# State-space stage of a hybrid decoder layer: B is turned on VectorE in the wide stage and loaded turned, instead of being turned on TensorE in each step

## The chip, the cores and the metric

The kernel runs on one core of one Trainium2 chip. A core has a matrix engine (TensorE, "PE" in the profile, with its weight loads as "PEld"), a vector engine (VectorE, "DVE"), an engine for activations and scaled copies (ScalarE, "ACT"), a general engine (GpSimd, "POOL"), a sequencer that here only issues DMAs (SyncE, "SP"), and 16 DMA engines between them. Each engine works through its own queue in order; semaphores connect the queues. ScalarE also issues DMAs, and each of these takes a place in its queue. The metric is the device time of one execution in microseconds; less is better.

## The reference

One layer over a sequence of S = 1024 positions and D = 1024 channels in float32. A normalised and modulated input `h` is multiplied by one wide matrix `w_in`; its columns feed a chunked gMLP mixer, a Mamba-2 state-space mixer and two gates. The part that matters here:

```
proj = h @ w_in
gm_u, gm_v, gm_z, ssm_z, xbc, dt_raw, g_a, g_b = split(proj)
xbc = silu(causal_depthwise_conv(xbc, conv_w, conv_b))      # 4 taps
xs, bm, cm = split(xbc)                                     # x: 2048, B: 8*128, C: 8*128
# state space, per chunk of 128 positions, 8 groups of 4 heads:
cb           = einsum('bclgn,bcsgn->bcgls', cc, bc)
y_diag       = einsum('bcgls,bcgrls,bcsgrp->bclgrp', cb, decay, xd)
chunk_states = einsum('bcsgn,bcgrs,bcsgrp->bcgrpn', bc, decay_to_end, xd)
state        = state * chunk_decay + chunk_states
y_off        = einsum('bclgn,bcgrpn,bcgrl->bclgrp', cc, prev_states, exp(a_cs))
y_b = rms_norm((y_diag + y_off + x * d_skip) * silu(ssm_z))
merged = sigmoid(g_a) * (y_a @ w_proj_a) + sigmoid(g_b) * (y_b @ w_proj_b)
out = rms_norm(x + gate * (merged @ w_out))
```

B (`bc`) is used in two ways. In `cb` it is contracted over its 128 states `n`; in `chunk_states` it is contracted over the 128 positions `s` of a chunk. TensorE contracts over partitions, so the first needs B with states on the partitions, and the second needs it with positions on the partitions: B turned.

## The kernel before, in words

**The wide stage** (about 160 to 870 us) computes `proj` with channels on the partitions, in pairs of 128 columns. A pair is seven products of half-size blocks (`p1` to `p7`), each of twelve matmuls of 128x512, since every float32 operand is split in a high and a low part and three of the four partial products are taken. ScalarE and VectorE take the products out of PSUM into tiles `c1` and `c2` of 128x1024. The order of the pairs is `cb0, uz0, x0, uz1, cb1, uz2, x1, uz3, cb2, uz4, x2` and so on. The products of one pair are interleaved with the last of the pair ahead: after `p1` and `p5` of the new pair comes `p4` of the old one.

When both halves of a tile are complete, the pair's `done` function runs. For the channels of the convolution it is `conv_done(i, g, r)`: ScalarE scales the tile `cc` into a new tile `ac`, VectorE adds the three delayed taps, ScalarE applies SiLU, and a DMA on ScalarE's queue stores `ac` in the DRAM tile `s_d[g]`. The index `r` says which of the six parts of a group's tile it is: 0 for C, 1 for B (tile `c2cb<g>`), 2 and 3 for x, and 4 and 5 for the gate z. Tiles of 128x1024 (`wide`) come from one rotation with tag `w4` of 6 buffers, so a new tile waits until the last reader of the tile six before it is done. `later(k, f, ...)` runs `f` k products later.

**The state-space stage** (about 910 to 1100 us) has 32 steps, two groups in alternation, each a group `g` and a pair of chunks `s`. SP loads the decays (`dcy`) and the group's six parts (`sl`) about four steps ahead (`fetch`). `mask` and `decay` build the masked exponentials on ScalarE (`ea`, `dcy`) and POOL. `prep` runs two steps ahead on TensorE. For each of the two chunks it makes C·B into the bank `pc`, turns B into the other half of `pc`, and turns x into the bank `px`; VectorE then multiplies `dcy` by C·B, and makes `xd` and `xe` from `px`; ScalarE copies turned B to `bn`. `front` makes the products `yi` (from `dcy` and `xd`) and the state `sp` (from `bn` and `xe`). `back` makes `yn` from C and the state. VectorE and POOL add and gate the result, and ScalarE's queue stores it. Between the steps TensorE draws from another supply of matmuls (`pma`, the projection `y_a @ w_proj_a`). Within the stage, `link("A" / "V" / "G", ...)` chains the instructions of ScalarE, VectorE and POOL in the order of the code, and `mm`, `tp` and `load` keep TensorE and SP in the order of the code. Elsewhere a scheduler sets the order of ScalarE and VectorE.

## Time and profile before

| what | value |
|---|---|
| median of 3 runs | 1362.2 us (1361.05 to 1365.36) |
| the profiled execution | 1362.27 us |
| its span in the trace | 1360.4 us |
| TensorE busy | 1347.0 us, 99% of the span |
| VectorE, ScalarE, POOL busy | 1056.1, 800.4, 196.1 us |
| DMA packets | 249577, 288.64 MB, mean 212 GB/s |

The span runs from the first to the last recorded instruction; the time of an execution is 1.87 us longer. Busy times are the time in which at least one instruction of an engine was under way. TensorE's matmuls overlap, so a single one's duration is longer than its share of the queue; that share is the distance from its start to the next start. `waits` in the profile are idle times of an engine and the event that ended them.

### The profile page before, as it was taken

How to read it: one execution, taken by the hardware profiler on the slowest of the kernel's cores; microseconds unless marked ns; L12 is line 12 of the kernel's file. 1: busy time of each engine (PE TensorE's matmuls, PEld its weight loads, DVE VectorE, ACT ScalarE, POOL GpSimd, SP SyncE). 2: the span in 40 equal slices, each digit the busy share in tenths (PEclk: the TensorE clock that was granted, in tenths of full speed). 3: DMA queues.
4: the chain of work that ended last, by engine and by line, in shares of the span. 5: the costliest groups of instructions: out<-in, count | busy, mean ns of one | idle time of the engine just before them, and what ended most of it. 6: DMA issues, size and time to landing. Idle time of an engine off the chain costs nothing.

```text
span 1360.4 us, 20108 instructions
## 1 busy us (share of the span) xinstructions
PE 1347.0 (99%) x6907; PEld 1114.4 (82%) x6907; DVE 1056.1 (78%) x1731; ACT 800.4 (59%) x1446; POOL 196.1 (14%) x193
## 2 busy tenths in 40 slices
PE   8999999999999999999999999999999999999997
PEld 6688888888888888888888888888888888888886
DVE  4776786787777898688887788358888877959976
ACT  5754666666657665466576655486877834233453
POOL 1000000000000000000000000007798981000002
PEclk9999999999999999999999999999999999999999
DMA  9675444333345667777656866489889878888913
GB/s 292 177 248 142 134 124 124 117 119 122 101 132 155 193 184 231 248 216 246 202 192 193 244 204 186 154 289 318 302 297 311 306 256 291 313 261 317 381 45 124
DMA packets 249577, 288.64 MB, mean 212 GB/s; under 512 B 16860, under 2 KB 196484, under 8 KB 249476
## 3 DMA queue, kind: packets, MB, share of 16 engines
q1 hardware_dynamic: 174868, 203.80, 47.0%
q10 hardware_dynamic: 74544, 83.57, 18.0%
q8 instruction: 54, 0.88, 0.3%
q14 instruction: 47, 0.39, 0.1%
q0 software_dynamic: 64, 0.00, 0.0%
HBM read 199.82 MB, written 87.49 MB: 211 GB/s over the span
## 4 chain that ended last, share of the span: by engine, by line
PE 93%; POOL 3%; DMA 1%; issue 1%; ACT 1%; DVE 1%; SPq 0%; POOLq 0%; DVEq 0%; ACTq 0%
PE xcb L585 6%; PE xz L585 6%; PE xuz L585 6%; PE xx L585 6%; PE xg L585 6%; PE pma L82 5%; PE ox L1914 3%; PE yuz L585 3%; PE yx L585 3%; PE ycb L585 3%; PE yp L1722 3%; PE yz L585 3%; PE vx L990 3%; PE yg L585 3%; PE oy L1914 2%; PE x0p L1722 2%
## 5 line engine op out<-in xcount | busy, mean ns | idle before, releaser
L1159 POOL TENSOR_SCALAR_AFFINE_SELECT dcy<-dcy 128x1024 f32<-128x1024 f32 x32 | 35.3, 1103 | 788.7 <-ACT ea L1155 788.7
L1167 ACT ACTIVATE dcy<-dcy,nacs 128x128 f32<-128x128 f32 x256 | 78.3, 389 | 2.9 <-POOL dcy L1159 2.4
L1183 DVE TENSOR_TENSOR dcy<-dcy,pc 128x1024 f32<-128x1024 f32 x32 | 39.0, 1218 | 8.0 <-PE pc L85 5.8
L1265 POOL TENSOR_TENSOR yz<-y,sl 128x512 f32<-128x512 f32 x32 | 44.7, 1396 | 2.5
L82 PE MATMUL pma<-yh,wah 128*128 128x512 f32 x128 | 43.2, 418 | 0.0
L82 PE MATMUL pma<-yh,wal 128*128 128x512 f32 x128 | 42.6, 413 | 0.0
L82 PE MATMUL pma<-yl,wah 128*128 128x512 f32 x128 | 40.2, 395 | 0.0
L1155 ACT ACTIVATE ea<-dcy 64x512 f32<-64x512 f32 x64 | 39.8, 622 | 0.4
L1190 ACT COPY bn<-pc 128x256 f32<-128x256 f32 x32 | 11.9, 371 | 46.4 <-DVE dcy L1183 44.9
L1060 ACT ACTIVATE ac<-ac 128x1024 f32<-128x1024 f32 x32 | 33.9, 1060 | 8.1 <-DVE ac L1058 7.9
L1264 POOL TENSOR_TENSOR y<-y,ym 128x512 f32<-128x512 f32 (+1 forms) x32 | 37.4, 1170 | 1.8 <-DVE ym L1262 1.8
L1058 DVE SCALAR_TENSOR_TENSOR ac<-c2x,cwt,ac 128x1023 f32<-128x1023 f32 (+2 forms) x24 | 30.7, 1278 | 8.8 <-ACT ac L1056 8.7
L1058 DVE SCALAR_TENSOR_TENSOR ac<-c2cb,cwt,ac 128x1023 f32<-128x1023 f32 (+2 forms) x24 | 30.7, 1278 | 8.2 <-ACT ac L1056 8.0
L1929 POOL TENSOR_TENSOR r<-r,fnw 128x512 f32<-128x512 f32 x4 | 6.1, 1534 | 207.3 <-ACT junk L1927 207.3
L82 PE MATMUL yi<-dcy,xd 128*64 128x128 f32 x512 | 35.0, 279 | 0.0
L1262 DVE TENSOR_TENSOR ym<-yn,ea 128x512 f32<-128x512 f32 (+1 forms) x32 | 19.9, 621 | 18.2 <-PE yn L82 18.0
L1653 DVE SCALAR_TENSOR_TENSOR yn<-yn,par,rb 128x512 f32<-128x512 f32 x32 | 26.1, 822 | 9.1 <-DMA yn<-yb_d 9.1
L82 PE MATMUL sp<-xe,bn 128*128 128x256 f32 x112 | 32.7, 409 | 0.0
L82 PEld LDWEIGHTS yn<-sl,st 128*128 128x128 f32 x224 | 29.8, 191 | 2.8 <-POOL st L1228 0.4
L82 PEld LDWEIGHTS yi<-dcy,xd 128*64 128x64 f32 x512 | 27.3, 136 | 5.7 <-issue 3.2
L1058 DVE SCALAR_TENSOR_TENSOR ac<-c1cb,cwt,ac 128x1023 f32<-128x1023 f32 (+2 forms) x24 | 30.6, 1276 | 1.3 <-ACT ac L1056 1.3
L1022 ACT ACTIVATE vm<-vm,vr 128x128 f32<-128x128 f32 x64 | 25.5, 483 | 10.1 <-DMA vm<-v_d 9.6
(2983 smaller groups left out, 4368.4 us busy)
## 6 DMA issues: line engine op xcount, KB each, us to landing
sl<-s_d SPq DMA_DIRECT2D x32, 768.0 KB
s_d<-ac ACTq DMA_DIRECT2D x32, 512.0 KB
wb_d<-wbb ACTq DMA_DIRECT2D x32, 512.0 KB
dcy<-acs_d SPq DMA_DIRECT2D x32, 512.0 KB
av<-in_w_in_dram SPq DMA_DIRECT2D x36, 256.0 KB
aw<-in_ada_w_dram SPq DMA_DIRECT2D x16, 512.0 KB
wbr<-in_w_proj_b_dram SPq DMA_DIRECT2D x32, 256.0 KB
yb_d<-yz ACTq DMA_DIRECT2D x32, 256.0 KB
```

Of the source, the lines that this page charges most:

```text
L82: pin(PE.matmul(acc, l, r, start=first, stop=last))
L585: pin(PE.matmul(ps, lw[:, k * P : (k + 1) * P], r[k], start=first and n + k == 0, stop=n == 2 and k == 3, skip_group_check=not first))
L990: pin(PE.matmul(ps[pn][j], l[:, j * P : (j + 1) * P], r, start=nm in ("p1", "p5", "p2") and n + units[i][1] == 0, stop=n == 2 and k == 3, ...
L1058: V.scalar_tensor_tensor(ac[:, s:], cc[:, : S - s], conv_wt[:, 3 - s, i : i + 1], ac[:, s:], op0=ALU.mult, op1=ALU.add)
L1155: link("A", lambda: A.activation(ea[hh * HD : (hh + 1) * HD], dcy.rearrange("p (j e) i l -> p e j (i l)", e=2)[hh * HD : (hh + 1) * HD, hh ...
L1159: link("G", lambda: G.affine_select(out=d8, in_=d8, compare_op=ALU.is_ge, fill=-1e30, base=0, pattern=[[0, 2 * HPG], [1, P]], channel_mult ...
L1167: link("A", lambda: A.activation(dcy[:, h, i, :], dcy[:, h, i, :], AF.Exp, bias=sub[:, i, h : h + 1]))
L1183: link("V", lambda: V.tensor_tensor(d3, d3, pc[:, 0:256].unsqueeze(1).to_broadcast([P, HPG, 256]), op=ALU.mult))
L1264: link("G", lambda: G.tensor_add(y1[:, :, t0:], y1[:, :, t0:], m[:, :, t0:]))
L1265: link("G", lambda: G.tensor_mul(yz, y1, sl[:, 4:6]))
L1722: pin(PE.matmul(ps[j], a[:, v, js], r, start=first and n + k == 0, stop=n == 2 and k == KT - 1, skip_group_check=not first))
L1914: pin(PE.matmul(ps, a[:, tsl], b[:, cs], start=first and n + j == 0, stop=n == 2 and j == 3, skip_group_check=not first))
```

## The change

`conv_done` for B starts a task one product later. VectorE turns the finished tile `ac` in blocks of 32x32 into the tile `cc`, whose contents are no longer needed. Block (a, b) of 32 states and 32 positions is turned in its place, so four DMAs on ScalarE's queue, one for each 32 partitions, put the blocks where they belong in the new DRAM tile `bt_d[g]`; each moves 32 partitions x 32 blocks x 32 numbers, in runs of 128 bytes. In the state-space stage SP loads `bn` from `bt_d` with positions on the partitions, up to four steps ahead, ahead of that round's `fetch`. TensorE's turns of B and ScalarE's copies of them leave `prep`.

```
+    bt_d = [dt_([NCH, 4, 32, P], f"bt_d{g}") for g in range(NG)]
...
             store(s_d[g][:, :, r, :], ac.rearrange("p (s t) -> p s t", s=4))
+            if r == 1:
+                later(1, turned, g, cc, ac)
         return done
+
+    def turned(g, cc, ac):
+
+        V.transpose(cc, ac)
+        for n in range(4):
+            ns = slice(32 * n, 32 * n + 32)
+            store(bt_d[g].rearrange("c b t n -> t (c b) n")[:, :, ns], cc[ns].rearrange("p (b n) -> p b n", n=32))
...
+        def turned(self, s):
+            bn = p2x.tile([P, 2, P], F32, name=f"bn{self.g}_{s}", tag="bn", bufs=3)
+            load(bn, bt_d[self.g][2 * s : 2 * s + 2].rearrange("c b t n -> (b t) c n"))
+            self.bn[s] = bn.rearrange("p c n -> p (c n)")
...
                 mm(pc[:, i * P : (i + 1) * P], sl[:, 1, tsl], sl[:, 0, tsl])
-                tp(pc[:, 256 + i * P : 256 + (i + 1) * P], sl[:, 1, tsl], ident)
                 tp(px[:, i * 256 : i * 256 + P], sl[:, 2, tsl], ident)
...
-            bn = p2x.tile([P, 256], F32, name=f"bn{nm}", tag="bn", bufs=3)
-            link("A", lambda: A.copy(bn, pc[:, 256:512]))
-            self.pre[s] = (sl, dcy, bn, xs[0], xs[1], ea)
+            self.pre[s] = (sl, dcy, self.bn.pop(s), xs[0], xs[1], ea)
...
+    def turned_b(n):
+        while done_t[0] < min(n, len(order)):
+            g, s = order[done_t[0]]
+            groups[g].turned(s)
+            done_t[0] += 1
...
     def start_ssd():
         fetch(2)
+        turned_b(3)
...
             step(n + 2, "prep")
+        turned_b(n + 4)
         fetch(n + 6)
```

Three places show what moves in the queues. The first is TensorE in the preparation of group 0's second pair of chunks (`pc0_1`, `px0_1`), before:

```order
L82 MATMUL yn0_0_8445<-sl0_0_7907,st_8258 128x128 x2
L82 MATMUL pc0_1_8454<-sl0_1_8264 128x128
L85 MATMUL pc0_1_8454<-ident_135,sl0_1_8264 128x128
L85 MATMUL px0_1_8453<-ident_135,sl0_1_8264 128x128 x2
L82 MATMUL pc0_1_8454<-sl0_1_8264 128x128
L85 MATMUL pc0_1_8454<-ident_135,sl0_1_8264 128x128
L85 MATMUL px0_1_8453<-ident_135,sl0_1_8264 128x128 x2
L82 MATMUL yn1_0_8475<-sl1_0_7912,st_8258 128x128 x2
```

The same place after:

```order
L83 MATMUL yn0_0_8491<-sl0_0_7955,st_8304 128x128 x2
L83 MATMUL pc0_1_8500<-sl0_1_8310 128x128
L86 MATMUL px0_1_8499<-ident_143,sl0_1_8310 128x128 x2
L83 MATMUL pc0_1_8500<-sl0_1_8310 128x128
L86 MATMUL px0_1_8499<-ident_143,sl0_1_8310 128x128 x2
L83 MATMUL yn1_0_8519<-sl1_0_7960,st_8304 128x128 x2
```

The two turns into `pc` are gone; the rest of TensorE's order is the same in the whole kernel.

The second place is ScalarE in the wide stage behind group 2's convolution of B (`ac18`, from the tile `c2cb2`), where the pair x2 begins (`c1x2`, `p5x2`) while the pair uz4 ends, before:

```order
L1060 ACTIVATE ac18_3160<-ac18_3160 128x1024
L571 CAST p7x2h_3096<-a21x2_3063 128x512
L94 DMA s_d2_123<-ac18_3160 512x1x256
L1041 ACTIVATE c1uz4_3130<-c1uz4_3130 128x1024
L571 CAST p4x2h_3100<-a22x2_3065 128x512
L601 COPY c2uz4_3231<-xuz4_3104 128x512
L571 CAST p1uz5h_3249<-a11uz5_3234 128x512
L601 COPY c1x2_3293<-xx2_3277 128x512
L571 CAST p5uz5h_3253<-s1uz5_3242 128x512
L601 COPY p5x2_3308<-yx2_3295 128x512
```

And after:

```order
L1061 ACTIVATE ac18_3178<-ac18_3178 128x1024
L572 CAST p7x2h_3114<-a21x2_3081 128x512
L95 DMA s_d2_123<-ac18_3178 512x1x256
L1042 ACTIVATE c1uz4_3148<-c1uz4_3148 128x1024
L572 CAST p4x2h_3118<-a22x2_3083 128x512
L95 DMA bt_d2_131<-c2cb2_3076 32x32x32
L602 COPY c2uz4_3254<-xuz4_3122 128x512
L95 DMA bt_d2_131<-c2cb2_3076 32x32x32 x3
L572 CAST p1uz5h_3272<-a11uz5_3257 128x512
L572 CAST p5uz5h_3276<-s1uz5_3265 128x512
L602 COPY c1x2_3316<-xx2_3300 128x512
L602 COPY p5x2_3331<-yx2_3318 128x512
```

The four stores stand ahead of the copy of `xx2` into `c1x2`, and that tile takes over the buffer of `c2cb2`, which the stores read.

The third place is SP in the state-space stage, around the loads for group 1's third and group 0's fourth pair of chunks, before:

```order
L91 DMA tha1_0_8435<-th_d_111 128x512
L91 DMA tha1_1_8438<-th_d_111 128x512
L91 DMA dcy1_2_8470<-acs_d_57 128x1024
L91 DMA sl1_2_8472<-s_d1_122 128x1536
L91 DMA dcy0_3_8508<-acs_d_57 128x1024
L91 DMA sl0_3_8510<-s_d0_121 128x1536
```

And after:

```order
L92 DMA tha1_0_8481<-th_d_111 128x512
L92 DMA tha1_1_8484<-th_d_111 128x512
L92 DMA bn1_1_8512<-bt_d1_130 128x2x128
L92 DMA dcy1_2_8514<-acs_d_57 128x1024
L92 DMA sl1_2_8516<-s_d1_122 128x1536
L92 DMA bn0_2_8548<-bt_d0_129 128x2x128
L92 DMA dcy0_3_8550<-acs_d_57 128x1024
L92 DMA sl0_3_8552<-s_d0_121 128x1536
```

One load of turned B stands ahead of each step's two loads.

4 lines of the change are left out of this document (2 added, 2 removed).

## The prediction, made before the changed kernel ran

> **What bounds the kernel now.** I read the page's busy times and its chain first, then the windows by stage, then the weight-load waits inside the state-space stage.
>
> ```profile
> PE 1347.0 (99%) x6907; PEld 1114.4 (82%) x6907; DVE 1056.1 (78%) x1731; ACT 800.4 (59%) x1446; POOL 196.1 (14%) x193
> ```
>
> ```profile
> PE 93%; POOL 3%; DMA 1%; issue 1%; ACT 1%; DVE 1%; SPq 0%; POOLq 0%; DVEq 0%; ACTq 0%
> ```
>
> TensorE carries 93% of the chain that ended last. The change touches two stages, so I take those two windows (columns: sum, PE, PEld, DVE, ACT, POOL busy, clock, DMA share, GB/s).
>
> ```profile
> 160.00:870.00 710.00, 710.00 (x3210) 590.47 (x3209) 556.22 (x850) 438.28 (x672) 0.00 (x0) 1.00 0.56 173
> 910.00:1100.00 190.00, 189.85 (x1488) 160.97 (x1487) 159.72 (x280) 141.44 (x374) 155.64 (x152) 1.00 0.89 308
> ```
>
> In the wide stage (160 to 870) TensorE never stops; VectorE has 154 us to spare, ScalarE 272 us, and the DMA engines are half idle. In the state-space stage (910 to 1100) TensorE is idle 0.15 us of 190, while POOL (82%), VectorE (84%) and DMA (0.89) are all close behind. So an instruction that leaves TensorE there shortens the stage by its step, as long as none of the three takes over.
>
> **The turns that go.** The group of B's turns, and one step's preparation on TensorE in order of time:
>
> ```profile
> L85 PE MATMUL pc<-ident,sl 128*128 128x128 f32 x64 | 17.4, 273 | 0.0
> ```
>
> ```profile
> 1002.47 0.39 PE L82 MATMUL pc<-sl 128*128 128x128 f32 x2
> 1002.69 0.27 PE L85 MATMUL pc<-ident,sl 128*128 128x128 f32 x1
> 1002.80 0.38 PE L85 MATMUL px<-ident,sl 128*128 128x128 f32 x2
> 1003.02 0.39 PE L82 MATMUL pc<-sl 128*128 128x128 f32 x2
> ```
>
> The 273 ns are a pipelined duration. What a turn takes from the queue is the distance to the next start: 1002.80 - 1002.69 = 0.11 us. (The pair of x turns agrees: 0.22 us for two.) 64 turns x 0.11 = 7.04 us, which is 0.22 us for each of 32 steps. The group's 17.4 us of busy time overlap their neighbours and would overstate it.
>
> A little more may go with them. The weight loads of the matmuls behind the preparation wait for it:
>
> ```profile
> PEld yi L82 <- PE pc L85: 1.9, 11, 0.2
> ...
> PEld yn L82 <- POOL st L1228: 0.4, 1, 0.4
> ```
>
> At most 1.9 us, at least nothing, since the x turns still stand ahead of the same loads. I take 0.5: only 11 of several hundred loads show it.
>
> **The copies that go.**
>
> ```profile
> L1190 ACT COPY bn<-pc 128x256 f32<-128x256 f32 x32 | 11.9, 371 | 46.4 <-DVE dcy L1183 44.9 <-DMA wa<-in_w_proj_a_dram 1.4
> ```
>
> ScalarE loses 11.9 us of copies and the 44.9 us in which they waited for VectorE's product of decays and C·B. That ends no wait of TensorE, so I count 0 directly. But the next mask and decays stood behind that wait, and POOL waits for ScalarE's `ea` ahead of its mask:
>
> ```profile
> POOL dcy L1159 <- ACT ea L1155: 40.1, 20, 18.6
> ```
>
> Part of these 40.1 us (18.6 of it one wait at the start) should come forward. VectorE's operations in the step stay as they are.
>
> **The turns on VectorE (wide stage).** 8 block transposes of 128x1024 float32. No such instruction ran before. Nearest row of the same engine and shape:
>
> ```profile
> L1042 DVE TENSOR_TENSOR ya<-c1uz,ya 128x1024 f32<-128x1024 f32 x8 | 9.8, 1220 | 0.0
> ```
>
> I take 1.22 us each, 9.8 us in all, with bounds of half and double (0.61 to 2.4). A pair of products there lasts about 19 us and leaves VectorE some 4 us; one transpose falls into eight pairs only. Cover: TensorE's 710 of 710 busy us do not wait on VectorE. If that cover were gone it would cost up to 9.8 us. I count 0.
>
> **The stores on ScalarE's queue.** 32 stores of 128 KB, each 1024 runs of 128 bytes. Issuing first (least, median and longest ns):
>
> ```profile
> L94 ACTq DMA_DIRECT2D s_d<-ac x32: 520/527/646, 169.2 to 844.8; - x32
> L94 ACTq DMA_DIRECT2D wb_d<-wbb x32: 362/366/1503, 453.4 to 835.3; - x32
> ```
>
> 32 x 0.37 to 0.53 = 12 to 17 us, four at a time: 1.5 to 2.1 us by which ScalarE's next PSUM copy is late, eight times. A product lasts 2.7 us (rows below) and a bank is wanted again about two products later, so 5.4 us are there and a copy takes 0.6: hidden, 0.
>
> The packets are the unknown. Larger packets, tiny ones, and a busy stretch of 128-byte broadcasts, each as packets and the queue's share of 16 engines' time, in windows 109 to 150, 1138 to 1142 and 103 to 106 us:
>
> ```profile
> DMA packets 15159, 8.44 MB, mean 206 GB/s; under 512 B 518, under 2 KB 14901, under 8 KB 15157
> ...
> q1 hardware_dynamic: 6842, 4.28, 36.9%
> q10 hardware_dynamic: 8315, 4.13, 34.1%
> ```
>
> ```profile
> q10 hardware_dynamic: 146, 0.00, 2.1%
> ```
>
> ```profile
> q1 hardware_dynamic: 414, 0.08, 12.4%
> ```
>
> Mostly 512-byte packets: 0.71 x 41 us x 16 / 15157 = 31 ns each. 32-byte stores: 0.021 x 4 x 16 / 146 = 9 ns. 128-byte reads: 0.124 x 3 x 16 / 414 = 14 ns busy; but as throughput only 414 arrived in 3 us, 3 x 16 / 414 = 116 ns each. That is the upper bound, 9 ns the lower. I take 25 ns, between the row of equal size and the row of 512 bytes: 64 packets per engine and store make 1.6 us, a group's four 6.4 us. All 32768 then take 51 us of queue (18 to 238), in a stage whose DMA share is 0.56 of 710.
>
> [...]
>
> **Who waits for these stores.** The tile that they read is a buffer of a rotation. In groups 0, 1, 3, 4, 6 and 7 the next user stands some 12 to 19 instructions later on its engine. Group 2 is tightest: ScalarE's `COPY c1x` for pair x2 takes over that buffer right behind. The place before:
>
> ```profile
> 342.69 0.60 ACT L571 CAST p4x2h<-a22x 128x512 fp32r<-128x512 f32 x1
> 343.20 0.58 ACT L601 COPY c2uz<-xuz 128x512 f32<-128x512 f32 x1
> 343.83 0.63 ACT L571 CAST p1uz5h<-a11uz 128x512 fp32r<-128x512 f32 x1
> 344.73 0.59 ACT L601 COPY c1x<-xx 128x512 f32<-128x512 f32 x1 [0.28 <-PE xx L585]
> ```
>
> ```profile
> 349.07 1.07 PE L585 MATMUL xuz<-t4h,p4uz4l 128*128 128x512 f32 x4
> 349.97 0.84 PE L585 MATMUL xx<-t2h,p6x2h 128*128 128x512 f32 x3
> ```
>
> TensorE adds to that bank from 349.97 on (four matmuls in 0.90 us, so a product of twelve in 2.7), so the copy may be 4.6 us late. Four stores go out from about 343.3 to 345.2; a large store shows what landing costs:
>
> ```profile
> ACT wbb L860 <- DMA wb_d<-wbb: 14.8, 10, 4.0
> ```
>
> Waits up to 4.0 us. From 343.3 + 6.4 us of queue + about 1 to 2 us of flight I get 350.7 to 351.7, plus the copy of 0.6: a stall of 1.3 to 2.3 us at 25 ns; none at 14 ns (3.6 us of queue); at 116 ns (29.7 us) about 25 us, and other groups join. ScalarE's copy of the other product is queued behind it and follows at once. I count +1.0, between none and 2.3.
>
> **The loads of turned B.** 32 loads of 128 KB in 512-byte runs on SP's queue, each put ahead of the decays' and sl's loads of a later step:
>
> ```profile
> L91 SPq DMA_DIRECT2D sl<-s_d x32: 319/320/730, 870.2 to 1086.7; - x32
> ```
>
> ```profile
> 1026.74 0.37 SPq L91 DMA_DIRECT2D dcy<-acs_d  x1
> ```
>
> ```profile
> 1033.32 1.25 ACT L1155 ACTIVATE ea<-dcy 64x512 f32<-64x512 f32 x2
> ```
>
> An issue is 0.32 us, the load is asked for two steps or more before its matmul, and `dcy` loads lead their first reader by 6.6 us here. Its packets add 256 per step over 16 engines at 31 ns: 0.5 us. Cover 6.6, so 0. Three of them stand ahead of the stage and delay the mixer's loads by a microsecond of issue: 0.
>
> What it does to the DMA engines and to POOL:
>
> ```profile
> DMA packets 25889, 58.48 MB, mean 308 GB/s; under 512 B 3596, under 2 KB 10812, under 8 KB 25866
> ```
>
> ```profile
> 910.00:920.00 10.00, 10.00 (x68) 7.84 (x67) 9.30 (x15) 6.95 (x18) 1.55 (x2) 1.00 1.03 388
> ...
> 1010.00:1020.00 10.00, 10.00 (x79) 8.38 (x76) 8.12 (x16) 7.83 (x22) 9.84 (x9) 1.00 0.78 271
> ...
> 1040.00:1050.00 10.00, 9.85 (x82) 8.22 (x83) 8.61 (x17) 6.38 (x18) 9.84 (x10) 1.00 0.89 302
> ```
>
> 29 loads of 131 KB make 62.3 MB; in 183 us that is 340 GB/s, where a full stretch has reached 388. [...]
>
> POOL is 9.84 of 10 us busy in some windows, so a 10 us stretch there can give back 0.16 instead of 0.4 (0.22 per step of 5.5 us). Two are shown; taking three such, 3 x 0.24 = 0.7. Earlier masks work against it, so I count +0.5.
>
> **Sum.** 1362.27 (the profiled execution: span 1360.4 and 1.87 around it; 0.1 above the median of 1362.2) - 7.0 - 0.5 + 1.0 + 0.5 = 1356.3.
>
> **Rivals.** About 0.3% (4.1 us) is what a measurement can tell from no change.
>
> 1. Slow small stores. One mechanism: a store of 1024 short runs holds the buffer until it has landed. By the sum for group 2 (343.3 + 256 packets + 2.1, against 349.97) the stall is 7.5 us at 47 ns a packet, and from there the gain is used up; from 63 ns, with a stall of 11.6, the kernel is slower by 0.3%. At 116 ns: 1362.3 - 7.5 + 25 = 1380 for group 2 alone, more if the other seven groups follow. For it: the 116 ns. Against it: 9, 14 and 31 ns as busy time. Chance 0.19.
>
> 2. The state-space stage finds another bound: POOL in all windows, or DMA. If the stage moves 325 GB/s at best, 62.3 MB take 192 us instead of 183, and the time is 1356.3 + 9 = 1365; with half of that, 1361. For it: DMA 0.89 and POOL up to 9.84 of 10. Against it: no wait of TensorE but 0.4 us, 388 GB/s reached, earlier masks. Chance 0.23.
>
> 3. The turns go, nothing else shows: 1362.3 - 7.0 to - 8.9 = 1353.4 to 1355.3. This is the good end of my forecast.
>
> The forecast, 1353.4 to 1358, has 0.58. For 8 in 10 the range runs from 1353.0 to 1366, which takes in rival 2 and the mild part of rival 1 (a stall of up to 11 us). Faster 0.58, same 0.23, slower 0.19.
>
> **What would show it.** TensorE's matmuls down by 64 and the stage from 910 to 1100 shorter by about 7 us at the same start-to-start steps; no `bn` copy on ScalarE, and less of POOL's wait for `ea`. In the wide stage: eight transposes near 1.2 us, no TensorE idle beyond 1 to 2 us near 350. Wrong would be: idle TensorE behind a `c1x`, `c2z` or `c1z` copy that waits for a store of turned B (rival 1), or waits of `sp` for the turned-B load and of `yn` for POOL (rival 2).

## The result, and the profile after

The changed kernel takes 1373.05 us (median of 6 runs, 1370.93 to 1373.9) against 1361.84 of the kernel before (6 runs on the same chip). The ratio is 1.0076, with a 95% interval of 1.0063 to 1.0089: slower by 0.8%, where 1356.3 us and "faster" had been forecast, with 1366 us as the upper end of the range. The profiled execution took 1372.28 us, 10.0 us more than the profiled execution before (1362.27); its span is 1370.6.

The page of the changed kernel, its busy times and its chain:

```profile
PE 1343.1 (98%) x6843; PEld 1106.0 (81%) x6843; DVE 1063.2 (78%) x1739; ACT 785.7 (57%) x1414; POOL 195.3 (14%) x193
```

```profile
PE 69%; DMA 9%; DVE 7%; issue 4%; ACT 4%; POOL 4%; SPq 1%; ACTq 1%; POOLq 0%; DVEq 0%
```

TensorE has lost exactly its 64 turns (6907 to 6843 matmuls) and 3.9 us of busy time, and yet the span has grown by 10.2. TensorE's share of the chain that ended last has fallen from 93% to 69%, and other engines and DMAs stand in it now: TensorE waits. The windows of the two stages, moved by the delay at their edges (columns as in the prediction):

```profile
160.00:879.00 719.00, 712.77 (x3205) 588.93 (x3204) 563.19 (x858) 431.62 (x671) 0.00 (x0) 1.00 0.59 176
918.00:1106.00 188.00, 183.67 (x1429) 154.86 (x1428) 160.02 (x281) 134.06 (x345) 153.55 (x152) 1.00 0.96 327
```

Before, TensorE had no idle time in the first and 0.15 us in the second. Now it is idle for 6.2 us in the wide stage and 4.3 us in the state-space stage, whose DMA share has gone from 0.89 to 0.96. The waits of TensorE in the changed kernel (line, what it waited for, us in total, times, longest); before, not one of these stood in the list:

```profile
PE pq L83 <- POOL yz L1305: 4.3, 3, 1.8
PE x3p L1742 <- DVE tha L1545: 3.0, 1, 3.0
...
PE xuz L586 <- ACT c2uz L602: 1.8, 1, 1.8
...
PE xg L586 <- ACT c1g L602: 1.3, 1, 1.3
...
PE xx L586 <- ACT c2x L602: 0.9, 1, 0.9
PE xcb L586 <- ACT c1cb L602: 0.8, 1, 0.8
...
PE xz L586 <- ACT c2z L602: 0.5, 1, 0.5
PE xx L586 <- ACT c1x L602: 0.5, 1, 0.5
```

The order of TensorE's matmuls is the same in both kernels but for the 64 turns. So each matmul of the one can be laid beside the same matmul of the other, and the difference of their start times is a ledger of where the 10 us came from:

| where | change, us |
|---|---|
| before the wide stage | -0.7 |
| wide stage: eleven stalls, the largest behind copies `c2uz` 2.0, `c1g` 1.6, `c2x` 1.2, `c1cb` 1.1, `c1x` 0.8 | +9.5 |
| state space: 64 turns, 0.22 for each step | -7.0 |
| state space: three waits of `pq` for POOL's sum | +4.3 |
| behind it: a wait of `x3p` for a PSUM bank, 3.2, and 1.5 of slow clock after it | +4.7 |
| the rest, to the end | -0.7 |
| sum | +10.1 |

(Where two kernels do the same, the ledger still drifts by up to 0.9 us, so smaller entries of one run are not read. A stall counts 0.2 to 0.3 us more in it than in the list of waits, since a pipelined matmul ends later than its share of the queue (0.39 us against 0.23 for those of `x0p`) and idle time is counted from that end.) The gain of the turns is there in full. Against it stand 9.5 us in the wide stage, for which the prediction had counted 1.0, and 9.0 us of waits in and behind the state-space stage, for which it had counted 0.5.

**The largest stall of the wide stage**, in time order. First ScalarE and VectorE of the changed kernel where the pair x1 begins (the copy `c2uz<-xuz` frees the bank that TensorE wants next), then TensorE:

```profile
264.55 0.62 ACT L572 CAST p1uz3h<-a11uz 128x512 fp32r<-128x512 f32 x1
266.54 1.61 ACTq L95 DMA_DIRECT2D bt_d<-c2cb  x3
268.19 0.58 ACT L602 COPY c2uz<-xuz 128x512 f32<-128x512 f32 x1 [3.01 <-DVE ya L1043]
```

```profile
265.27 1.24 DVE L1069 STREAM_TRANSPOSE c2cb<-ac 128x1024 f32<-128x1024 f32 x1
266.43 1.18 DVE L1043 TENSOR_TENSOR ya<-c1uz,ya 128x1024 f32<-128x1024 f32 x1
```

```profile
268.83 1.20 PE L586 MATMUL xuz<-t4h,p4uz2h 128*128 128x512 f32 x4 [1.82 <-ACT c2uz L602]
```

ScalarE is idle from 265.2: the first store waits for the transpose, which ends at 266.51. Three stores then leave one after the other until 268.15, and only then can the copy behind them in the queue start. The profile names VectorE's `ya` as what ended the wait (its buffer is the one that `c2uz` takes over), but `ya` was done at 267.61; the stores were last, by 0.5 us. So two things hold the copy, and by these rows the stores alone account for 0.5 us of TensorE's wait of 1.8: the rest is VectorE's `ya`, which now stands behind the transpose (e5 below has this place without the stores). The same place before:

```profile
265.20 0.58 ACT L601 COPY c2uz<-xuz 128x512 f32<-128x512 f32 x1
```

```profile
267.49 1.07 PE L585 MATMUL xuz<-t4h,p4uz2h 128*128 128x512 f32 x4
```

There the copy ended at 265.78 and the bank was wanted at 267.49: 1.7 us of slack. It did not wait for `ya`, which began only at 265.44.

### The profile page after: what moved, and what is told of

It reads as the page before. It is cut to its first block, busy times and chain, and to the rows that moved or that the text cites. A ratio compares the mean times of both kernels' runs of the same rounds, so it can differ in the third digit from the quotient of the medians.

```text
span 1370.6 us, 20090 instructions
## 1 busy us (share of the span) xinstructions
PE 1343.1 (98%) x6843; PEld 1106.0 (81%) x6843; DVE 1063.2 (78%) x1739; ACT 785.7 (57%) x1414; POOL 195.3 (14%) x193
## 4 chain that ended last, share of the span: by engine, by line
PE 69%; DMA 9%; DVE 7%; issue 4%; ACT 4%; POOL 4%; SPq 1%; ACTq 1%; POOLq 0%; DVEq 0%
PE xuz L586 5%; PE xx L586 5%; PE xcb L586 4%; PE pma L83 4%; PE xz L586 4%; PE ox L1934 3%; PE vx L991 3%; PE yp L1742 3%; PE xg L586 3%; PE yuz L586 2%; PE yx L586 2%; PE oy L1934 2%; DMA wb_d<-wbb 2%; PE ycb L586 2%; PE yz L586 2%
## 5 line engine op out<-in xcount | busy, mean ns | idle before, releaser
L861 ACT CAST wbb<-wbr 128x512 fp32r<-128x512 f32 x32 | 19.8, 620 | 33.8 <-DMA wb_d<-wbb 28.1
L866 DVE TENSOR_TENSOR wbb<-wbr,wbb 128x512 fp32r<-128x512 f32 x32 | 21.9, 684 | 12.1 <-ACT wbb L861 12.1
```

## The experiments

Three questions: what in the wide stage costs 9.5 us, what in the state-space stage gives 9.0 back, and whether there is a version that keeps the gain. Each run is compared with the kernel before on the same chip. "Wide" and "state" are the changes in the ledger over the wide stage (160 to 870 of before) and from there to the end.

| run | what it has | time, us | ratio (95%) | wide | state |
|---|---|---|---|---|---|
| the change | all | 1373.05 | 1.0076 (1.0063 to 1.0089) | +9.5 | +1.3 |
| e1_wide | wide part alone | 1369.75 | 1.0056 (1.0041 to 1.0071) | +7.1 | -0.9 |
| e3_turn | transposes alone | 1362.07 | 1.000 (0.999 to 1.001) | +0.5 | -0.8 |
| e4_store | stores alone | 1361.81 | 1.000 (0.9991 to 1.001) | 0.0 | -0.9 |
| e7_touch | transposes, ScalarE waits, no stores | 1364.13 | 1.0017 (1.0006 to 1.0028) | +2.8 | -0.1 |
| e10_runs | wide part, long runs | 1365.39 | 1.0024 (1.0014 to 1.0033) | +4.0 | -0.9 |
| e5_pool | all, stores on POOL's queue | 1370.32 | 1.0056 (1.0034 to 1.0078) | +7.1 | -0.6 |
| e6_sp | all, stores on SP's queue | 1388.69 | 1.0178 (1.0141 to 1.0215) | +22.7 | -3.3 |
| e2_state | state part alone | 1364.68 | 1.002 (1.0005 to 1.0035) | 0.0 | +0.9 |
| e18_noload | the same, `bn` loaded once | 1369.42 | 1.0057 (1.0042 to 1.0072) | 0.0 | +6.9 |
| e8_bank | all, two banks exchanged | 1367.63 | 1.0036 (1.002 to 1.0051) | +7.8 | +0.7 |
| e12_state | state part, three repairs | 1364.78 | 1.0018 (1.0007 to 1.0028) | 0.0 | +3.2 |
| e13_sum | state part, sum earlier | 1366.05 | 1.0033 (1.0024 to 1.0043) | 0.0 | -1.0 |
| e14_early | the same, banks chosen anew | 1360.82 | 0.9995 (0.9985 to 1.0004) | 0.0 | -5.3 |
| e16_wah | the same, casts in fixed order | 1359.17 | 0.9962 (0.9948 to 0.9976) | 0.0 | -2.6 |
| e19_noload | the same, `bn` loaded once | 1361.99 | 1.0002 (0.9992 to 1.0012) | 0.0 | -0.9 |
| e11_all | all, five repairs | 1372.77 | 1.0075 (1.0048 to 1.0103) | +6.6 | +1.5 |
| e15_full | all, e14's repairs | 1366.42 | 1.0033 (1.0021 to 1.0045) | +7.5 | -2.7 |
| e17_long | all, e16's repairs, long stores | 1362.18 | 0.9993 (0.9981 to 1.0005) | +1.6 | -4.6 |

The ledger is of one profiled execution, the time a median; where a kernel's runs spread (e2: 1358.5 to 1368.3; e6: 1381.1 to 1391.9; e8: 1362.9 to 1373.2; e13: 1362.3 to 1368.8; e14: 1357.1 to 1364.6), the two need not agree; the profiled execution is the fastest one in e1, e4, e5, e6, e13, e14 and e17. The kernel before takes 1361.6 to 1362.0 us in the median beside all of these runs but e16 and e17; on their chip it takes 1364.75 (17 runs, 1361.0 to 1366.7), so their ratios are not to be set beside the others. Diffs below are against the changed kernel unless another is named.

### Half the change at a time: e1_wide, e2_state

e1 keeps the wide part and goes back to TensorE's turns; nothing reads the stored B.

```
+                tp(pc[:, 256 + i * P : 256 + (i + 1) * P], sl[:, 1, tsl], ident)
...
-            self.pre[s] = (sl, dcy, self.bn.pop(s), xs[0], xs[1], ea)
+            bn = p2x.tile([P, 256], F32, name=f"bn{nm}", tag="bn", bufs=3)
+            link("A", lambda: A.copy(bn, pc[:, 256:512]))
+            self.pre[s] = (sl, dcy, bn, xs[0], xs[1], ea)
...
-        turned_b(3)
-        turned_b(n + 4)
```

> The wide stage's part alone: VectorE's turns and the 32 stores stay, but nothing reads bt_d, and the state-space stage turns B on TensorE as before. Queue theory (the stores stand in ScalarE's queue, wait there for the turn, and each takes 0.3 to 2.8 us to issue, so that copies out of PSUM behind them are late): TensorE loses the 9.4 us that it lost in the wide stage of the changed kernel, the rest is as before, 1362.2 + 9.4 = about 1371. Packet theory (short runs hold the DMA engines): the same sum. Against both, that the loss comes about only together with the state-space part: within 2 us of 1362.

e2 keeps the state-space part; the wide stage is that of before.

```
-            if r == 1:
-                later(1, turned, g, cc, ac)
...
-            load(bn, bt_d[self.g][2 * s : 2 * s + 2].rearrange("c b t n -> (b t) c n"))
+            load(bn, gm_ws[2 * s : 2 * s + 2].rearrange("c t n -> t c n"))
```

> The state-space stage's part alone: no turns and no stores in the wide stage; bn is loaded from the input gm_ws, which has the same 128x2x128 shape in runs of 512 bytes, so the products with B's turn are made of other numbers. Theory of the ledger: the turns bring -7.0, three waits of the row sums pq for POOL cost +4.2 again, and the wait of x3p for tha with the slow clock behind it +4.2 again: 1362.2 + 1.4 = about 1363.6. Rival, that these two losses come from the wide stage's shifted order or from the traffic of B's real tile: 1355.

The wide part alone costs 7.7 us (1369.75 against 1362.01), the state-space part alone costs 2.7 (1364.68). Both are losses, and their sum, 10.4, is near the whole (11.2). So the two stages can be taken apart, though not wait by wait: the wait for `wah` below is not in the changed kernel's list. TensorE's new waits in e2:

```profile
PE pq L83 <- POOL yz L1303: 3.0, 3, 1.1
PE pma L83 <- ACT wah L1432: 2.6, 1, 2.6
PE x3p L1740 <- DVE tha L1543: 2.0, 1, 2.0
```

The 7.0 us of the turns are in its ledger too; these 7.6 us take them back. Of the two forecasts the rival's (1355) is out, and with it the idea that these losses come from the wide stage or from B's real tile.

### The wide part in pieces: e3_turn, e4_store, e7_touch, e10_runs

e3 is e1 without the 32 stores; e4 is e1 without the transposes, so that the stores take the unturned tile.

```
-        for n in range(4):
-            ns = slice(32 * n, 32 * n + 32)
-            store(bt_d[g].rearrange("c b t n -> t (c b) n")[:, :, ns], cc[ns].rearrange("p (b n) -> p b n", n=32))
```

> VectorE's eight turns alone, without the stores; the state-space stage as before. Queue theory and packet theory: no TensorE wait, 1362 within 1 us. Order theory (the eight extra instructions make the scheduler set weight preparation elsewhere in the queues of ScalarE and VectorE, and its waits hit copies out of PSUM): stalls from 480 us on remain, 1364 to 1367.

```
-        V.transpose(cc, ac)
```

> The 32 stores alone, of the tile c2cb as it is (not turned), at the same place; the state-space stage as before. They wait for no turn. Queue theory: the issuing of four stores (about 2 us, more where one takes 2.8) remains, the wait of about 1.2 us for the turn goes: 4 to 8 us of the 9.4 remain, 1366 to 1370. Packet theory: all of the 9.4 remain, 1371. Order theory: no clear forecast.

Neither costs anything; for e4 both theories had forecast a loss. The transposes are as forecast, and free by themselves (e3; columns: count, busy us, mean ns, idle before):

```profile
L1069 DVE STREAM_TRANSPOSE c2cb<-ac 128x1024 f32<-128x1024 f32 x8 | 9.9, 1237 | 0.0
```

In e3 the copies take over other buffers: at the place shown above `c2uz` waits for the transpose alone and starts at 266.38, in time, so e3 does not test what `ya` costs there. The 32768 packets of 128 bytes and their 32 issues are free as well, as long as nothing holds the stores up: the issues take as long in e4 (0.62 us in the median, 3.19 at most) as in the changed kernel. (Without the transpose the scheduler puts them some 13 to 23 us earlier in ScalarE's queue, so e4 does not test them at their place.) In the changed kernel's trace a packet of 128 bytes (these stores) took 13 ns in the median, one of 512 bytes (loads) 27, so about twice as long for a byte. e4 shows that this costs this kernel no time by itself.

e7 is e1 with four small copies on ScalarE, which wait for the transpose at the stores' place, instead of the stores. e10 is e1 with stores of the same bytes, each as 32 runs of 4096 bytes.

```
-            ns = slice(32 * n, 32 * n + 32)
-            store(bt_d[g].rearrange("c b t n -> t (c b) n")[:, :, ns], cc[ns].rearrange("p (b n) -> p b n", n=32))
+            A.copy(cc[:, 256 * n : 256 * n + 128], cc[:, 256 * n : 256 * n + 128])
```

> No stores: in their place four copies of 128x128 on ScalarE, of the turned tile onto itself, which wait for the turn as the stores do and stand at the same places in ScalarE's order; the state-space stage as before. It has the wait for the turn (about 1.2 us and more where VectorE is late) and about 1.1 us of ScalarE's time in place of some 2 us of issuing, and no DMA. If the wait for the turn is what costs: the stalls at c2uz (2.0) and part of the others stay, 1364 to 1368. If it is the issuing of stores, their landing or the DMA queue: within 1 us of 1362.

```
-            store(bt_d[g].rearrange("c b t n -> t (c b) n")[:, :, ns], cc[ns].rearrange("p (b n) -> p b n", n=32))
+            store(bt_d[g].rearrange("c b t n -> (c b t n)").rearrange("(p x) -> p x", p=P)[ns], cc[ns])
```

> As the run of the wide part alone (turns and stores on ScalarE's queue, nothing reads bt_d), but each of the four stores writes its 32 partitions as 32 runs of 4096 bytes instead of 1024 runs of 128: same bytes, same number of stores, same place, same wait for the turn. bt_d then holds the tile unsorted. If the number of runs is what costs (issues of 0.3 to 2.8 us, landing late): the 7.7 us of that run go, 1362 to 1364. If the wait for the turn in ScalarE's queue and the held buffers cost, whatever the runs: 1367 to 1370.

Waiting for the transpose in ScalarE's queue, without a DMA, costs 2.4 us (1364.13 against 1361.73). Stores with long runs make it 3.5, and the short runs 7.7. So, if such differences may be read as parts, 2.4 of the 7.7 us are the wait and the order, 1.1 are stores at all, and 4.2 are the short runs. (The three runs do not stall at the same copies, so the parts are rough.) What short runs change is seen at the issue (least, median and longest ns; the changed kernel, then e10):

```profile
L95 ACTq DMA_DIRECT2D bt_d<-c2cb x32: 326/633/2840, 190.7 to 822.4; - x32
```

```profile
L95 ACTq DMA_DIRECT2D bt_d<-c2cb x32: 308/440/1408, 191.6 to 817.7; - x32
```

A store of 1024 short runs holds ScalarE's queue for 0.63 us in the median and for up to 2.84, not for 0.37 to 0.53. ScalarE in the changed kernel before the stall behind `c1g`:

```profile
705.82 2.26 ACTq L95 DMA_DIRECT2D bt_d<-c2cb  x2
...
708.12 2.84 ACTq L95 DMA_DIRECT2D bt_d<-c2cb  x1
711.00 0.59 ACT L602 COPY c2z<-xz 128x512 f32<-128x512 f32 x1 [4.15 <-issue]
711.03 0.94 ACTq L95 DMA_DIRECT2D bt_d<-c2cb  x1
...
715.72 0.57 ACT L602 COPY c1g<-xg 128x512 f32<-128x512 f32 x1
```

Four stores take from 705.82 to 711.97, 6.2 us, and the copies behind them are late. A second way would be late landing. ScalarE's waits for it in the wide stage (160 to 870), before and after, and SP's:

```profile
ACT wbb L860 <- DMA wb_d<-wbb: 14.8, 10, 4.0
```

```profile
ACT wbb L861 <- DMA wb_d<-wbb: 28.1, 13, 6.1
...
ACT c1x L602 <- DMA bt_d<-c2cb: 2.8, 1, 2.8
```

```profile
SPq L92 <- DMA bt_d<-c2cb: 16.6, 7, 12.1
```

ScalarE waits longer for the other stores of its queue to land (28.1 us instead of 14.8), and SP, which loads weights into the buffers that the stores read, waits 16.6 us for their landing. But this does not tell short runs from long ones: with long runs (e10) the two are 25.4 and 15.1 us, and in e4, which costs nothing, SP waits 14.5. That these waits cost TensorE anything is not shown, but for one copy. The one `c1x` that the prediction had singled out waits 2.8 us for its store, and costs TensorE 0.8: forecast +1.0.

### The stores on another queue: e5_pool, e6_sp

```
-            store(bt_d[g].rearrange("c b t n -> t (c b) n")[:, :, ns], cc[ns].rearrange("p (b n) -> p b n", n=32))
+            nc.gpsimd.dma_start(bt_d[g].rearrange("c b t n -> t (c b) n")[:, :, ns], cc[ns].rearrange("p (b n) -> p b n", n=32))
```

> The whole change, with the 32 stores of turned B on POOL's queue, which does nothing in the wide stage. Runs, packets and the turns stay. Queue theory (the wide stage loses because the stores wait for the turn and are issued in ScalarE's queue, ahead of copies out of PSUM): the 9.4 us of the wide stage go, 1373.05 - 9.4 = about 1363.6; only the c1x2 copy can still wait for the landing, +1. Landing theory (buffers and SP's weight loads are held until the short runs have landed, whichever queue they come from): 4 to 7 us of it stay, 1368 to 1371.

In e6 `load(...)`, on SP's queue, stands in that place.

> The whole change, with the 32 stores on SP's queue, pinned there in the order of the code. ScalarE's queue is free of them, but SP's weight loads behind them wait for the turn and four issues each time (some 2 to 4 us). Queue theory: SP runs 10 to 25 us ahead, so most of that is hidden, 1364 to 1366. Landing theory: 1368 to 1371.

With the stores on POOL's queue, which is empty in this stage, all stalls from 450 to 700 us are gone. So those came from the stores' place in ScalarE's queue. What is left is larger at fewer places:

```profile
PE xx L586 <- ACT c1x L602: 2.4, 1, 2.4
PE xuz L586 <- ACT c2uz L602: 1.2, 1, 1.2
PE xg L586 <- ACT c2g L602: 1.0, 1, 1.0
```

The wide stage still loses 7.1 us instead of 9.5, and the time of 1370.32 is in the range of the landing theory. One stall, though, is neither issue nor landing. It is the place shown above, where no store stands in ScalarE's queue any more:

```profile
267.61 0.59 ACT L602 COPY c2uz<-xuz 128x512 f32<-128x512 f32 x1 [2.45 <-DVE ya L1043]
```

The copy starts as VectorE's `ya` ends (267.57), and TensorE still waits 1.2 us. So at this place the transpose costs time, by what it delays in VectorE's queue and by the buffer that `c2uz` now takes over. On SP's queue the stores are worse by 15.6 us: SP stands still for the transpose, and the weights behind them come late, as SP's and VectorE's waits show:

```profile
SPq L92 <- DVE c2cb L1069: 183.0, 7, 36.8
```

```profile
DVE s1uz L575 <- DMA a22uz<-in_w_in_dram: 32.4, 6, 8.9
```

Both forecasts for e6 were too low. So the three queues differ in who is hurt, and none is free.

### Are the loads to blame in the state-space stage? e18_noload, e19_noload

The second rival of the prediction was that the 4.2 MB of added loads crowd out the others. e18 is e2 with one load of `bn` for all 32 steps; e19 does the same to e16 (below).

```
+            if not one_bn:
+                bn = p2x.tile([P, 2, P], F32, name="bn", tag="bn", bufs=1)
+                load(bn, gm_ws[:2].rearrange("c t n -> t c n"))
+                one_bn.append(bn.rearrange("p c n -> p (c n)"))
+            self.bn[s] = one_bn[0]
```

> The state-space part alone, as in the run that reads a stand-in for turned B, but that stand-in is loaded once ahead of the stage and used by all 32 steps: the 31 other loads of 128 KB (4.1 MB of about 62) are gone. The DMA share of the stage was 0.89 before and 0.96 with the loads, and ScalarE, which had waited for no load of the gate before, waited for loads there. Theory A, the loads crowd out the others: without them the DMA share is about 0.90, TensorE's waits for POOL's sum (3.0 us) and for the cast of the projection's weight (2.6) are gone or below 1 us together, only the bank wait of about 2 us is left, and the time is about 1357 us (7.0 less, 2.0 more). Theory B, the stage is only shorter and its fixed order no longer fits: the waits stay as they were, 5 to 8 us in all, and the time is 1362 to 1365 us.

> The same edit on the repaired state-space part (banks chosen anew, POOL's sum two products earlier, the first casts of the projection's weight in ScalarE's fixed order), which took 1359.2 us with its loads. Theory A, the loads crowd out the others: the waits of 3.3 us that the repaired version kept (for VectorE's and POOL's state) go, and the time is 1355 to 1356 us. Theory B, only the order matters: 1358 to 1360 us, as before this edit.

The DMA engines of e18 are as free as before the change (the window from 910 to 1098):

```profile
910.00:1098.00 188.00, 182.18 (x1411) 152.89 (x1410) 154.91 (x275) 130.96 (x338) 150.13 (x148) 0.99 0.89 303
```

And the waits are no shorter in sum (9.3 us against 7.6 in e2); they stand elsewhere:

```profile
PE yn L83 <- DVE st L1248: 4.4, 3, 1.9
PE x3p L1743 <- DVE tha L1546: 3.1, 1, 3.1
...
PE pq L83 <- POOL yz L1305: 1.4, 1, 1.4
```

Theory A, the loads, falls: without them both kernels are slower, e18 by 4.7 us (1369.42 against 1364.68) and e19 by 2.8 (1361.99 against 1359.17, on different chips; 1.7 in the ledger), not faster by 3 to 8. Theory B's direction holds, but not its size: 1369.4 lies above its 1362 to 1365, and 1362.0 above its 1358 to 1360. What the two runs say is that a load more or less moves the waits about. That the fixed order in four queues is the reason is likely, but not shown; and as taking the loads away shifts the order too, what a load costs by itself stays open.

### The waits of the state-space stage one by one: e8_bank, e12_state, e13_sum, e14_early, e16_wah

**`x3p` and its bank.** The eight accumulators of the stage behind take PSUM banks from a pool, in the order in which they are asked for and the banks come free. In the changed kernel the bank that `x3p` gets is one that VectorE's `tha` still reads; that `pc`, without ScalarE's copy, is free earlier is the likely reason. e8 exchanges two places in that order:

```
-                 first = {... for t in ('x0', 'x1', 'x2', 'x3', 'y3', 'y1', 'y2', 'y0')}
+                 first = {... for t in ('x0', 'x1', 'x2', 'y0', 'y3', 'y1', 'y2', 'x3')}
```

> The whole change, with the PSUM banks of the stage behind the state-space stage given out in another order (x3 and y0 exchanged), so that x3p no longer takes the bank that tha reads last. Theory: the 3.0 us wait of x3p goes, and with it the 1.2 us of slow clock behind it: 1373.05 - 4.2 = 1368.9. Rival (the tail of the state-space stage is late anyway, and the wait moves to x0p or to a later bank): 1372 to 1373.

The wait is gone, and 1367.63 us are 5.4 less than the whole change, with runs that spread by 10 us; its profiled execution is 1.9 less. In its profiled execution a wait for `wah` of 2.6 us stands in the list instead, as it does in e2's and not in the changed kernel's.

**`wah` and the mask.** The cast of the next projection weight, `wah`, stands in ScalarE's queue where the scheduler puts it: before, ahead of the decays of the fourth step; now behind them. Those decays wait for POOL's mask. ScalarE, POOL and VectorE in e2:

```profile
918.53 2.45 ACT L1180 ACTIVATE dcy<-dcy,nacs 128x128 f32<-128x128 f32 x8 [2.31 <-POOL dcy L1172]
```

```profile
916.29 2.21 POOL L1172 TENSOR_SCALAR_AFFINE_SELECT dcy<-dcy 128x1024 f32<-128x1024 f32 x1 [19.33 <-ACT ea L1168]
```

```profile
914.45 3.09 DVE L1415 TENSOR_TENSOR yl<-yl,yh 128x512 fp32r<-128x512 f32 x5
```

The mask takes 1.09 us in the median. Here it takes 2.21, and ends 1.0 us after VectorE's run of five `yl`, at 917.5: as if it had begun when that run ended. ScalarE's decays, and `wah` behind them, are late by so much.

e12 takes e2 with the exchanged banks, TensorE's product with POOL's sum (`pq`) two products later, and the cast at a higher priority of the scheduler:

```
-            later(2, posts.append, (self, q, sq[:1]))
+            later(4, posts.append, (self, q, sq[:1]))
...
-            A.copy(wh, wr)
+            with tc.high_priority():
+                A.copy(wh, wr)
```

> The state-space part alone (bn from gm_ws, no turns, no stores in the wide stage, so the products with B's turn are made of other numbers) with its own three losses undone: banks x3 and y0 exchanged, pq two products later, wah first. Theory: all 7.0 us of the turns remain as gain, 1362 - 7 = 1355. If POOL and ScalarE are the bound once TensorE is faster, the waits move to yn or yi and it stays at 1358 to 1362.

Nothing was won (1364.78 against e2's 1364.68), and neither forecast had that. The priority did not move the cast: it still stands behind the fourth step's decays (924.85 after 922.50). The wait of `x3p` and those for POOL's sum are gone, but `sp` waits now; that the later `pq` changed which bank each product gets is a guess:

```profile
PE sp L83 <- issue: 3.7, 3, 1.5
PE pma L83 <- ACT wah L1433: 2.6, 1, 2.6
```

**POOL's sum.** POOL's sum ahead of the first of the three waits, before and in the changed kernel:

```profile
1019.40 1.29 POOL L1293 TENSOR_TENSOR yz<-yz 128x512 f32<-128x512 f32 x1
```

```profile
1026.77 1.26 POOL L1305 TENSOR_TENSOR yz<-yz 128x512 f32<-128x512 f32 x1
```

Before, it ended 1.3 us ahead of its `pq` (1021.95). TensorE's start there has moved by 4.5 us without the wait, the sum's by 7.4: from the sum ahead of it (1008.30, now 1013.44) POOL took 11.1 us before and takes 13.3 now. It does not have more work between the two; it stands idle for ScalarE.

```profile
1016.79 1.09 POOL L1174 TENSOR_SCALAR_AFFINE_SELECT dcy<-dcy 128x1024 f32<-128x1024 f32 x1 [2.08 <-ACT ea L1170]
```

The two other late sums have such an idle time ahead of them too, 2.0 and 1.7 us, each ended by `ea`. (Idle times of this length stood elsewhere before, so their place matters and not their sum.) At the first place ScalarE was late since two squares of `yz` had waited 2.3 and 0.55 us for its own stores of `yz` to land; before, no square waited in this stage. At the second place the sum had been only 0.06 us ahead of `pq` before the change.

e13 is e2 with e8's banks, and has POOL make the sum two products earlier, while `pq` stays at its place in most groups (two products later behind an earlier sum):

```
-            work.append((slot[0] + 3, self.sum, q, sq))
+            work.append((slot[0] + 1, self.sum, q, sq))
-            later(2, posts.append, (self, q, sq[:1]))
+            later(4, posts.append, (self, q, sq[:1]))
```

> The state-space part alone (bn from gm_ws, no turns or stores in the wide stage), with the banks x3 and y0 exchanged and POOL's sums of squares two products earlier in its queue, while TensorE's order, the row sums pq among it, and with it the banks stay. Theory: of the run of the state-space part alone (1364.7, where pq cost 3.0, x3p 2.0 and wah 2.8) the first two go, 1359.7, and the wait for wah stays where POOL's third mask meets VectorE's run of yl. If POOL only passes the lateness on (the mask and y stand 1.3 us later behind the sum): waits of yi or yn instead, 1361 to 1364.

The waits for POOL are gone (the ledger stood at -5.2 us by 1100, from +0.8), but `x1p` now has the late bank: a wait of 4.0 us, and the clock of the profiled execution is 0.996 in the mean, against 0.998 in e2's. The median, 1366.05 us, is no better than e2's. e14 is e13 with the order `x0, y0, x2, x1, x3, y1, y2, y3`.

> As the run with POOL's sums earlier (the state-space part alone, bn from gm_ws), with the PSUM banks of the next stage given out so that x0 to x3 take none that tha reads last. Theory: the stage's 7 us of turns show at last: 1361.6 - 6 = 1355 to 1357 in executions in which POOL's third mask does not meet VectorE's run of yl, and 3 to 4 more in those in which it does; the median 1356 to 1360. If the state-space stage has another bound: 1361 to 1366 again.

With both repaired the profiled execution ends 5.3 us earlier than before in the ledger, at 1357.13 us. But it is the fastest of 12 by 2.9 us, the runs spread up to 1364.55, the median is that of before, and the other executions have no profile to say why. e16 links the first casts of `wah` into ScalarE's fixed order, ahead of the decays of the fourth step:

```
-            A.copy(wh, wr)
+            link("A" if dd == 1 else f"wah{dd}{i}", lambda: A.copy(wh, wr))
```

> As the run with sums earlier and banks chosen (state-space part alone, bn from gm_ws), and ScalarE's first two casts of wah linked into its chain, so that they stand ahead of the fourth step's decays, as they did before the change. Theory: the spread of that run (1357.1 to 1364.6) comes mostly from TensorE's wait for wah, behind decays that wait for POOL's long mask; with the casts ahead it goes: 1356 to 1358.5, and a smaller spread. If the mask's length itself delays TensorE another way (yi or yn): 1360 to 1361 again.

Now the spread is small (1357.5 to 1360.0, six runs), and the state-space part is faster: all six runs lie below the fastest of the kernel before on that chip (1361.0). By how much is less sure: the ratio of 0.9962 (0.9948 to 0.9976) says 5.2 us, against a kernel before that is slow on that chip; the ledger says 2.6. The mask took even longer in the profile:

```profile
913.80 3.76 POOL L1172 TENSOR_SCALAR_AFFINE_SELECT dcy<-dcy 128x1024 f32<-128x1024 f32 x1 [17.78 <-ACT ea L1168]
```

So 2.6 to 5.2 of the 7.0 us are to be had once the sum, the banks and the cast suit the shorter stage. In the profile waits of `sp` and `yn` for the state (2.0 and 1.3 us) take most of the rest.

### The whole change again: e11_all, e15_full, e17_long

e11 was tried ahead of e13: POOL's queue, e12's three repairs, and gate loads four products later (`later(72 + 10 * k, ...)`).

> The whole change with the losses found so far undone: the stores on POOL's queue; the gate's loads, which share the rotation of the wide tiles, four products later; the banks x3 and y0 exchanged; the row sums pq two products later; ScalarE's CAST of wah ahead of what else is ready. From 1370.3 (stores on POOL): c1x2's wait and slow clock -4.3, x3p -2.0, pq -1.6, wah -2.5: 1360, faster than before by 0.2%. If the losses only move to other waits: 1364 to 1369.

It gained nothing (1372.77, above both forecasts): the waits of e12, and in the wide stage `c2uz` 1.6 and `c2x` 2.0. e15 is the change with e14's two repairs.

> The whole change (turns and stores in the wide stage on ScalarE's queue, real turned B) with the same two repairs of the state-space stage: sums earlier, banks chosen. Theory: the wide stage's 7 to 9 us of loss stay, the state-space stage's 6 to 7 us of gain come: 1361 to 1365, no change against before. If the losses of both parts depend on each other: 1367 or more.

It takes 6.6 us less than the change. What is left is the wide stage, 7.5, and the wait for `wah`, 2.6, which is in its profile. e17 has e16's repairs and one store per group in runs of 4096 bytes; POOL's idle queue sorts it from DRAM to DRAM:

```
+    br_d = [dt_([P, S], f"br_d{g}") for g in range(NG)]
...
+        store(br_d[g], cc)
         for n in range(4):
             ns = slice(32 * n, 32 * n + 32)
-            store(bt_d[g].rearrange("c b t n -> t (c b) n")[:, :, ns], cc[ns].rearrange("p (b n) -> p b n", n=32))
+            nc.gpsimd.dma_start(bt_d[g].rearrange("c b t n -> t (c b) n")[:, :, ns], br_d[g][ns].rearrange("p (b n) -> p b n", n=32))
```

> The whole change, repaired: VectorE's turns stay; ScalarE issues one store of the turned tile in runs of 4096 bytes per group, and POOL's queue sorts the blocks from DRAM to DRAM into bt_d in four transfers of 128-byte runs, which hold no tile; in the state-space stage sums earlier, banks chosen, wah ahead. Theory: the wide stage then loses what the run with long runs lost, 3.4, or less (one issue in place of four), and the state-space stage gains 6 to 7: 1356 to 1359, faster than before by 0.2 to 0.4%. If the sorting or the wait for the turn costs as much as the four stores did: 1362 to 1366.

1362.18 us, ratio 0.9993 (0.9981 to 1.0005): 10.9 us less than the change, and no different from before; it fell in the rival's range. The wide stage loses 1.3 us at two `c2uz` copies (0.6 and 0.7), and the state-space part keeps 4.6 in the profile. It does the whole computation, and beats the change, but not the kernel before; no version here that does the whole work beat both.

## Why the prediction was wrong, step by step

- **The turns that go: -7.04 (0.11 each, 0.22 a step).** Right. TensorE's starts move by 0.11 at each of the 64 places, 7.0 us in all, in every run that has the state-space part. The 0.5 us of weight loads beside it did not show.
- **The transposes: 1.22 us, hidden.** Right in size: 1.237, and e3 costs nothing. Not hidden everywhere: its cover was that TensorE does not wait on VectorE, but a copy out of PSUM can. At the place of the largest stall `c2uz` now waits for `ya`, which stands behind the transpose, and TensorE waits for 1.2 us even with no store in ScalarE's queue (e5).
- **Issue of the stores: "hidden, 0".** This step failed. It took 0.37 to 0.53 us an issue from rows of other stores and set four of them against 5.4 us of slack. The issues took 0.63 in the median and up to 2.84, and the slack of the copy behind them was 1.7 us at `c2uz`, as the rows at 265.20 and 267.49 of the profile before would have told. And the step did not name what a store waits for. In an in-order queue, a store that waits for VectorE's transpose makes the copy behind it wait for VectorE too (transpose to 266.51, stores to 268.15, copy at 268.19). By e7, that wait and the order alone cost 2.4 us. In place of 0 the wide part costs 7.7 us (e1).
- **Who waits for the stores: +1.0 at `c1x2`.** Right at that place (0.8), but the claim that the other groups' buffers have 12 to 19 instructions to spare covered only the buffers, not the queue. A packet took 13 ns and not 25, but with what stood between them the packets of these four stores took 5.6 us (345.1 to 350.7), near the 6.4 counted; that 25 ns came so near is luck. The 1 to 2 us of flight were the author's estimate, and no row of before shows them by themselves; here the first packet came 0.9 us after the first store's issue began (344.18), and the copy (351.45) 0.8 us after the last packet.
- **The loads: 0.** Not refuted: e18 and e19 without them are no faster. The stage moved 327 GB/s at a share of 0.96, close to the 325 that the second rival assumed, and this looked like its proof; taking the loads away did not bear it out.
- **POOL: +0.5.** This step failed too: 4.3 us. The price was taken from POOL's idle share, in windows where it is busy for 9.84 of 10 us. That there are three waits is the number it had taken, by chance. What counts is how far ahead of `pq` the sum is done, and what POOL waits for: ahead of each late sum it was idle for 1.7 to 2.1 us, for ScalarE. The earlier masks that should have worked against it did not come as a whole: POOL was idle for 34.4 us of the stage before (190 - 155.64) and 34.5 after (188 - 153.55).
- **Not in the prediction at all:** the PSUM banks of the stage behind (4.7 with the clock), and the place of `wah` in ScalarE's queue, which the scheduler moved (2.6 in six of the variants, nothing in the profile of the change itself).
- **Rivals.** The first, slow stores, had the right side for the wrong reason: its mechanism was the time of a packet, 47 ns and more. A packet took 13 ns (22 with what stood between, in group 2), and e4 shows packets to cost nothing by themselves; short runs cost (4.2 us by e1 and e10) by what is queued behind them. Of the waits named as its signs only `c1x` waited for a store to land. Of the second, waits for POOL came, though of `pq` and not of `yn`, and the DMA is not shown to be a bound.

What stays open: how the short runs' 4.2 us come about, at ScalarE's issue or by late landing; e5 frees ScalarE, but its `c1x` and `c2g` stalls come in exchange. How much of the wide stage's 9.5 us comes by VectorE's queue, as at `c2uz`, is known for that one stall only. Why e18 and e19 are slower than e2 and e16 was not settled beyond their waits.

## What to carry over

Where one engine bounds a kernel and the others keep a fixed order, two engines can meet with hardly any slack (here 0.06 us at one of POOL's sums), and shortening the bound by 0.22 us a step turns such meetings into waits. So forecast the slack of each meeting (its producer's end against its consumer's start) and not the idle share of the producer. Of an instruction put into an in-order queue, ask what it will wait for and how long the next instruction behind it can be late, and ask it on both engines: here of the copies behind the stores and of `ya` behind the transpose. Measure a DMA's issue by a row with as many runs (here 0.63 us in the median with 1024 of them, 0.44 with 32 for the same bytes). And when a theory fits a utilisation (0.96 of the DMA engines), take the load away before believing it, and expect that to move the order as well.

## What the runs showed of the hardware that was not expected

**The clock after a short idle time.** In the changed kernel `x3p` waits 3.03 us; the matmuls behind it start 0.43 us apart instead of 0.23. The windows of 3 us show it in the column of the clock, the third from the end:

```profile
1132.00:1135.00 3.00, 0.30 (x2) 0.00 (x0) 3.00 (x7) 0.43 (x1) 1.73 (x2) 1.00 0.03 2
1135.00:1138.00 3.00, 2.66 (x6) 2.15 (x7) 3.00 (x6) 1.54 (x3) 0.61 (x1) 0.53 0.48 176
```

The clock stands at 0.5 for 3.41 us in the trace, from 1135.15, 0.2 us ahead of the end of the idle time, to 1138.57. It costs 1.5 us in the ledger. In e18 an idle time of 1.94 us ahead of 1005.95 was followed by a clock of 0.66; in e2 one of 1.99 us was not (1.00):

```profile
1006.00:1009.00 3.00, 3.00 (x22) 2.67 (x24) 2.62 (x5) 1.74 (x6) 2.67 (x4) 0.66 0.95 369
```

```profile
1127.00:1130.00 3.00, 2.03 (x9) 1.69 (x10) 3.00 (x6) 1.59 (x3) 1.66 (x1) 1.00 0.47 175
```

So about 2 us idle were followed by a slow clock once and not another time, and no run shows what decides it. The wait for `wah` takes 2.6 us at the same place in e2, e5, e8, e11, e12 and e15; the clock of the profiled execution is 0.996 in the mean in e8 and e12, and 0.998 in the other four. That fits a slow clock behind the wait in those two, but does not show its place. So a wait of 2 to 3 us can cost half as much again (1.5 us behind the 3.03), in some executions and not in others.

**VectorE's adds beside POOL's mask.** In e16 the mask of 1.09 us took 3.76 us, from 913.80 to 917.56, beside VectorE's five `yl` (two operands each), which ended at 916.6; in e2 it took 2.21. Each time it ended about 1.0 us after the run. Before, the mask came first (914.74, 1.09 us), and VectorE's four `yl` took 3.36 us where four of them had taken 2.49 a little earlier. In these three places the one that started later took longer, the mask by 1.1 us in e2 and 2.7 in e16, the four adds by 0.9 before. What held it up is not shown, and no run here tests this by itself.
